# Where the split weights lie in on-chip memory, relative to the activation tiles, in a one-core decoder layer

## The chip, the cores and the metric

The kernel runs on one core of a Trainium2 chip. The core has TensorE (PE, the matrix engine), VectorE (DVE), ScalarE (ACT), GpSimd (POOL) and SyncE (SP), which only issues transfers here. The metric is the device time of one execution in microseconds (us). Lower is better.

## The reference

One layer of a decoder: 512 tokens, model width 2,048, everything in 32-bit floats.

```
mod = silu(c) @ w_ada + b_ada                     # six shift/scale/gate vectors
h = rmsnorm(x, g_mix) * (1 + sc1) + sh1
proj = h @ w_in          # q,k,v of 8 stick-breaking heads; q,k,v of 8 sparse heads;
                         # index queries, index key, index weights; two gates of 2048
y_a = stick_breaking_attention(q_a, k_a, v_a) @ w_a
y_b = sparse_attention(rope(q_b), rope(k_b), v_b, top 128 by the indexer) @ w_b
x = x + (1 + gt1) * ((sigmoid(g_a) * y_a + sigmoid(g_b) * y_b) @ w_o)
h = rmsnorm(x, g_ffn) * (1 + sc2) + sh2
u = causal_conv_width_3(h @ w_up)                 # 2 x 5632 channels
out = rmsnorm(x + (1 + gt2) * ((silu(u_a) * u_b) @ w_down), g_final)
```

Nearly all arithmetic is in the products with `w_in`, `w_a`, `w_b`, `w_o`, `w_up` and `w_down`.

## The kernel before

**Products in three parts.** Every operand of a large product is split into two `float32r` parts, a high one and the rest (`parts`, line 131, for weights, giving `wh` on ACT at line 133 and `wl` on DVE at line 135; `split`, line 160, for activations, into slots of tag `F`). `mm3` (line 141) then issues three matmuls: high by high (line 143), high by rest (144), rest by high (145). The second argument of `mm` is the stationary operand (128 columns, loaded as weights into the array), the third the moving one (256 or 512 columns). The profile names a matmul as out<-moving,stationary.

**Three ways to use them.**
- *Strassen units with tokens as columns* (`unit`, line 207): 31 of them for most of `w_in`, 8 for `w_o`, 41 for `w_up`. A unit makes two output tiles of 512 tokens with seven products instead of eight. The weights' parts are stationary and the token forms (`f`, halves of F tiles) are moving, 256 columns at a time: 7 x 8 x 3 matmuls.
- *Weights stationary, 512 tokens moving*: the first query products (from line 389), the 80-column tail (line 460), `w_a` and `w_b` (lines 926 and 968), and the first sixteen steps of the up-projection (`plain`, line 1108; some of these go over 256 columns).
- *Tokens stationary, 512 columns of weights moving*: the values (lines 440 to 448 and `values`, line 669), and all of `w_down` (`plain_down`, line 1230, and `strassen_down`, line 1282, Strassen units with tokens as rows). The very last `w_down` rows are split into F tiles beforehand (line 1419), so that there both operands are F tiles.

**Buffers.** `sb.tile(..., tag=...)` takes a buffer of a tag; tiles with one tag take turns on its `bufs` buffers. The buffers of a pool lie one behind the other in the order in which the tags are first used, each start rounded up to 32 bytes; a pool's first byte is 16,512 per partition here. So a 4-byte tile pushes everything behind it by 32 bytes. Before the change `eps` (4 bytes) stands ahead of the large tags, and `c_col` (64 bytes) stands between `raw` and `wl`. Worked out from the sizes, in bytes past a multiple of 512:

| tag | before |
|---|---|
| `T`, `F` (62 buffers of 2,048), `raw` (8 of 4,096) | 288 (32 past a multiple of 128) |
| `wl`, `wh` (3 buffers of 4,096 each) | 352 (96 past a multiple of 128) |
| `const` (identity, ones, masks) | 128 |

The column blocks of a weights' part are 512 bytes apart and the halves of an F tile 1,024, so every matmul of a full block has its two operands 64 bytes apart, modulo 512, wherever one is a weights' part. The tail's blocks are 80 columns, 320 bytes, apart.

**Order.** The instructions of an engine run in the order of its queue; the builder orders them by program order as their inputs and buffers come free. `behind(p)` adds that what is issued inside comes after `p` on the same engine. The transfer of the convolution's weights (`cw`, line 1087) goes out on ACT's queue behind `sig`, the last sigmoid of the input projection. `macc` (line 283) takes the row sums of the `w_ada` products that DVE makes beside the matmuls (`ada_half`, line 287); its last readers are `ada_end` (line 306) near the end of the `w_o` units. `cw` and `macc` are separate buffers.

Of the kernel before, what the change touches and what calls it, by code (L numbers as in the profile page):

```python
# [10 lines left out]
F32 = mybir.dt.float32  # L11
F32R = mybir.dt.float32r
# [6 lines left out]
P = 128  # L19
D = 2048  # L20
S = 512
KT = D // P
# [54 lines left out]
def block_kernel(ctx: ExitStack, tc: tile.TileContext, A: dict, out: bass.AP):  # L77
    nc = tc.nc
    sb = ctx.enter_context(tc.tile_pool(name="sb", bufs=1))
    pp = ctx.enter_context(tc.tile_pool(name="pp", bufs=1, space=PSUM))  # L80
    dr = ctx.enter_context(tc.tile_pool(name="dr", bufs=1, space=bass.MemoryType.DRAM))

# [33 lines left out]
    b_ada = vec[:, :96]  # L116
    g_mix, g_ffn = (vec[:, 96 + i * KT : 96 + (i + 1) * KT] for i in range(2))
    mask = sb.tile([P, 2, P], BF16, tag="mask", name="mask")
    cw = sb.tile([P, 2 * NJ, 4], F32, tag="cw", name="cw")
    eps = sb.tile([P, 1], F32, tag="eps", name="eps")  # L120
    nc.vector.memset(eps, EPS)


# [4 lines left out]

    pins = {}

    def parts(raw, w=1024):
        wh = t2k("wh", 3, F32R, w)
        pins["wh"] = act(wh, raw, AF.Copy)  # L133
        wl = t2k("wl", 3, F32R, w)
        pins["wl"] = tt(wl, raw, wh.bitcast(F32), ALU.subtract)  # L135
        return wh, wl

# [69 lines left out]
    def unit(src, f, between=lambda *_: None, late=None):  # L207

        n = len(f)
        w = n * P
        bank = (acc, att)[units[0] % 2]
        units[0] += 1
        r1, r2, r3 = (bank()[:, :HALF] for _ in range(3))

        def product(ps, a, name, first, pairs=None):
            for p in pairs or range(n):  # L220
                last = mm3(ps, cols(a, p), f[p][name], first and p == 0, p == n - 1, check=False)
            return last

        a11 = load(src[0], w)
        a21 = load(src[2], w)
        a22 = load(src[3], w)
        a12 = load(src[1], w)
        product(r1, parts(a11, w), "B11", True)
        e = t2k("ta", 2)
        p1, p5 = e[:, :HALF], e[:, HALF:]  # L230
        act(p1, r1, AF.Copy)
        s = t2k("raw", 8, w=w)
        last_v = tt(s, a21, a22, ALU.add)  # L233
        product(r3, parts(s, w), "T1", True)
        last = act(p5, r3, AF.Copy)
        between(0, last, last_v)
        tt(s, s, a11, ALU.subtract)  # L237
        product(r2, parts(s, w), "T2", True)
        e = t2k("sp", 2)
        u2, u3 = e[:, :HALF], e[:, HALF:]  # L240
        last_v = tt(u2, r2, p1, ALU.add)
        if late:
            c1, c2 = slot(), slot()
            steps = late(c1, c2)
            tt(s, a12, s, ALU.subtract)
            tt(a11, a11, a21, ALU.subtract)
            tt(u3, p1, p5, ALU.add)
            product(r3, parts(s, w), "B22", False)
            b21 = parts(a11, w), parts(a12, w)
            tt(c1[:, HALF:], r3, u2, ALU.add)  # L250
            next(steps)
            product(r2, b21[0], "T3", False)
            t4 = parts(a22, w)
            next(steps)
            tt(c2[:, HALF:], r2, u3, ALU.add)
            next(steps)
            product(r1, b21[1], "B21", False)
            act(c1[:, :HALF], r1, AF.Copy)
            next(steps)
            at = n - n // 3 - 1  # L260
            with behind(product(r2, t4, "T4", False, range(at))):
                last = next(steps)
            with behind(last):
                product(r2, t4, "T4", False, range(at, n))
            tt(c2[:, :HALF], r2, p1, ALU.add)
            return c1, c2
        product(r1, parts(a12, w), "B21", False)
        c1, c2 = slot(), slot()
        last = act(c1[:, :HALF], r1, AF.Copy)
        between(1, last, last_v)  # L270
        tt(a11, a11, a21, ALU.subtract)
        product(r2, parts(a11, w), "T3", False)
        tt(u3, r2, p1, ALU.add)  # L273
        tt(c2[:, HALF:], u3, p5, ALU.add)
        tt(a12, a12, s, ALU.subtract)
        product(r3, parts(a12, w), "B22", False)
        tt(c1[:, HALF:], r3, u2, ALU.add)
        product(r2, parts(a22, w), "T4", False)
        tt(c2[:, :HALF], r2, p1, ALU.add)
        return c1, c2  # L280


    macc = sb.tile([P, 96, 2], F32, tag="macc", name="macc")
    mod = sb.tile([P, 96], F32, tag="mod", name="mod")
    amp = sb.tile([P, 2, KT], F32, tag="amp", name="amp")

# [37 lines left out]
        return cb  # L324

    cb = c_spread()
    c_col = sb.tile([P, KT], F32, tag="c_col", name="c_col")
    nc.scalar.dma_start(c_col, A["c_col"])
    act(c_col, c_col, AF.Silu)

# [1 line left out]
    def rms(squares, blocks=range(NQB), bank=outs):  # L332

        total = bank()
        at = slice(blocks[0] * P, (blocks[-1] + 1) * P)
        for b in blocks:
            for i, t in enumerate(squares):
                mm(total[:, b : b + 1], t[:, b * P : (b + 1) * P], ones[:, :1], start=b == blocks[0] and i == 0,
                   stop=i == len(squares) - 1, skip_group_check=True)
        r = sb.tile([P, NQB], F32, tag="r", bufs=2, name=nm("r"))  # L340
        rb = r[:, blocks[0] : blocks[-1] + 1]
        act(rb, total[:, blocks[0] : blocks[-1] + 1], AF.Sqrt, scale=1.0 / D, bias=eps)
        nc.vector.reciprocal(rb, rb)
# [145 lines left out]

    def rope_tables():  # L490
        f0, f1, f2, f3, f123, f23, fr = _turn_parts()
        inv = sb.tile([64, 1], F32, tag="inv", name="inv")
        nc.scalar.dma_start(inv, A["inv_freq"])
        pos = t2k("T", 2, I32)[:64]
        nc.scalar.dma_start(pos, A["positions"].to_broadcast([64, S]))
# [199 lines left out]
    def indexer():  # L695
# [6 lines left out]
        for b in range(NQB):  # L702
            nc.tensor.transpose(wps[:, b * IDXH : (b + 1) * IDXH], tail[IDXD:TN, b * P : (b + 1) * P],
                                ident[IDXD:TN, IDXD:TN])
        wi = sb.tile([P, NQB, IDXH], F32, tag="wi", name="wi")
        nc.vector.tensor_copy(wi.rearrange("p b h -> p (b h)"), wps[:, : NQB * IDXH])
        bias.extend(slot()[:, : (b + 1) * P] for b in range(1, NQB))
        yield
# [36 lines left out]
        for b in range(1, NQB):  # L745
            sc = bias[b]
            for i in range(TOPK // 8):
                m8 = sb.tile([P, 8], F32, tag="m8", bufs=2, name=nm("m8"))
                nc.vector.max(out=m8, in_=sc)
                nc.vector.match_replace(out=sc, in_to_replace=m8, in_values=sc, imm_value=TAKEN)  # L750
                if i % 2:
                    yield
            ts(sc, sc, TAKEN, NEG, ALU.not_equal, ALU.mult)
# [127 lines left out]
    ya = [split(o) for o in ya]  # L881

    def sparse_1(q, k):
        m = sb.tile([P, NQB], F32, tag="m", bufs=2, name=nm("m"))
        s = sb.tile([P, NQB], F32, tag="s", bufs=2, name=nm("s"))
        soft = sb.tile([P, 10 * P], F32, tag="soft", name=nm("soft"))
        lg = strips(*(acc() for _ in range(3)))
        p = strips(*of_soft(soft))
        for b in (2, 0, 1, 3):
            W = (b + 1) * P  # L890
            mm(lg[b], q[:, b * P : (b + 1) * P], k[:, :W], start=b > 0, stop=True, skip_group_check=True)
        for b in (2, 0, 1, 3):
            nc.vector.tensor_tensor_reduce(out=p[b], in0=lg[b], in1=bias[b], scale=HD**-0.5, scalar=-3.0e38,
                                           op0=ALU.add, op1=ALU.max, accum_out=m[:, b : b + 1])
        last = ts(m, m, -1.0, None, ALU.mult)
        for b in (2, 0, 1, 3):
            act(p[b], p[b], AF.Exp, bias=m[:, b : b + 1], accum_out=s[:, b : b + 1])
        return p, s, last
# [115 lines left out]
    def norm_late(c1, c2):  # L1014
# [1 line left out]
        c, sq = (c1, c2), (t2k("ta", 2), t2k("sp", 2))  # L1016
        total, rstd = att(), outs()
        wide = t2k("T", 2)
        r = sb.tile([P, NQB], F32, tag="r", bufs=2, name=nm("r"))

        def add_up(t, blocks, first=False):
            for b in blocks:
# [60 lines left out]
    rstd, finish_left, *left_norm = norm2  # L1083


    with behind(sig):
        nc.scalar.dma_start(cw, A["conv"])
    yd = [dr.tile([P, 2 * S], F32, tag=f"yd{j}", name=f"yd{j}") for j in range(NJ // 2)]
# [349 lines left out]
        return [fetch(x1t[:, t, b * S : (b + 1) * S]) for b in range(2, 4)]  # L1438

    def finish_tokens(t, xs, s):  # L1440
        r = sb.tile([P, NQB], F32, tag="r", bufs=2, name=nm("r"))
# [13 lines left out]
    for t in range(NQB):  # L1455
        ahead = operands(t + 1) if t + 1 < NQB else None
        xs = []
        s = sb.tile([P, NQB], F32, tag="s", bufs=2, name=nm("s"))
        for b in range(4):
            if not ps:  # L1460
                ps = bank(t)
# [126 lines left out]
```

## Time and profile before

| | |
|---|---|
| three runs | 2758.18, 2774.71, 2789.82 us (median 2774.71) |
| profiled execution, its own time | 2759.24 us |
| its span, first to last instruction | 2757.5 us |
| PE busy, matmuls | 2697.6 us (98%), 18,704 |
| weight loads busy | 2457.7 us (89%) |
| DVE busy | 2411.3 us (87%) |
| ACT busy | 1450.7 us (53%) |
| moved | 550.08 MB, 199 GB/s |
| mean granted TensorE clock | 0.995 |

Busy times of PE are modelled at the ends, since matmuls overlap; what one matmul costs in a dense stretch is the distance between the starts of two. The page's counts of PE are those of matmul records; a product of plain 32-bit floats has two, a `float32r` product one. Stages by time, roughly: first query products to 100 us, values to 192, tail and single tiles to 237, Strassen units of `w_in` to 855, indexer, values and attention to 1175, `w_b` to 1262, `w_o` to 1445, up-projection to 2292, `w_down` to the end.

### The profile page before, as it was taken

The numbers are of one execution on the slowest core, as the hardware profiler recorded it, in microseconds if no ns is written. First come the engines' busy times: TensorE is split into PE (matmuls) and PEld (weight loads), VectorE is DVE, ScalarE is ACT, GpSimd is POOL, SyncE is SP. The second block draws the span as 40 slices with busy tenths as digits, with TensorE's granted clock in tenths as the row PEclk, the third lists the DMA queues.
The fourth block names the chain that finished last, engine by engine and source line by source line (L and its number), as shares of the span: only waits on it lengthen the run. The fifth ranks groups of instructions, "written<-read, shape, count | busy, mean of one in ns | idle before, by whom it ended". The sixth has DMA issues, their size and how long they took to land.

```text
span 2757.5 us, 47708 instructions
## 1 busy us (share of the span) xinstructions
PE 2697.6 (98%) x18704; PEld 2457.7 (89%) x18704; DVE 2411.3 (87%) x3452; ACT 1450.7 (53%) x2045; POOL 315.3 (11%) x519
## 2 busy tenths in 40 slices
PE   8999999999999999999999999999999999999997
PEld 6779999999998777879999999999999998887876
DVE  8978979988887899889879999999999997888886
ACT  4444454455556655434557555555555555546452
POOL 0010000000012011111230000000000000002122
PEclk9999999999999999999999999999999999999998
DMA  9973456756567467865783566666666446569786
GB/s 348 354 254 122 156 181 195 232 176 188 166 195 238 133 206 243 279 213 174 233 269 108 179 176 178 187 177 184 176 179 182 130 131 219 151 176 245 193 256 196
DMA packets 164189, 550.08 MB, mean 199 GB/s; under 512 B 21414, under 2 KB 21798, under 8 KB 163964
## 3 DMA queue, kind: packets, MB, share of 16 engines
q1 hardware_dynamic: 116220, 405.34, 45.9%
q0 software_dynamic: 47152, 141.30, 18.4%
q8 instruction: 147, 2.41, 0.4%
q14 instruction: 78, 0.64, 0.1%
q10 hardware_dynamic: 592, 0.39, 0.1%
HBM read 453.71 MB, written 89.83 MB: 197 GB/s over the span
## 4 chain that ended last, share of the span: by engine, by line
PE 67%; DVE 8%; DMA 5%; issue 4%; ACT 1%; POOL 0%; DVEq 0%; POOLq 0%; ACTq 0%; SPq 0%
PE att L145 10%; PE att L143 10%; PE att L144 10%; PE acc L145 10%; PE acc L143 10%; PE acc L144 10%; DVE wl L135 3%; DMA raw<-in_w_x 1%; DMA raw<-in_w_down 1%; PE acc L722 1%; PE acc L816 1%; PE outs L922 1%; DMA raw<-in_w_o 1%; PE outs L145 1%; PE outs L144 1%
## 5 line engine op out<-in xcount | busy, mean ns | idle before, releaser
L133 ACT ACTIVATE wh<-raw 128x1024 fp32r<-128x1024 f32 (+2 forms) x792 | 828.9, 1053 | 962.2 <-DVE raw L237 179.1
L135 DVE TENSOR_TENSOR wl<-raw,wh 128x1024 fp32r<-128x1024 f32 (+2 forms) x792 | 952.6, 1210 | 126.5 <-ACT wh L133 121.8
L143 PE MATMUL acc<-F,wh 128*128 128x256 f32 (+1 forms) x2464 | 709.1, 290 | 12.8 <-ACT wh L133 7.1
L145 PE MATMUL acc<-F,wl 128*128 128x256 f32 (+1 forms) x2464 | 710.6, 289 | 6.1 <-DVE wl L135 6.1
L144 PE MATMUL acc<-F,wh 128*128 128x256 f32 (+1 forms) x2464 | 710.3, 288 | 0.6 <-DVE F L388 0.4
L143 PE MATMUL att<-F,wh 128*128 128x256 f32 (+1 forms) x2448 | 704.8, 289 | 5.8 <-DVE sp L273 4.5
L145 PE MATMUL att<-F,wl 128*128 128x256 f32 (+1 forms) x2448 | 704.2, 288 | 3.3 <-DVE wl L135 3.0
L144 PE MATMUL att<-F,wh 128*128 128x256 f32 (+1 forms) x2448 | 704.5, 288 | 1.2 <-DVE F L164 1.2
L143 PEld LDWEIGHTS acc<-F,wh 128*128 128x128 f32 x2464 | 463.3, 188 | 29.5 <-ACT wh L133 12.2
L145 PEld LDWEIGHTS acc<-F,wl 128*128 128x128 f32 x2464 | 463.0, 188 | 19.2 <-DVE wl L135 8.5
L143 PEld LDWEIGHTS att<-F,wh 128*128 128x128 f32 x2448 | 460.4, 188 | 19.3 <-ACT wh L133 5.2
L144 PEld LDWEIGHTS acc<-F,wh 128*128 128x128 f32 x2464 | 463.8, 188 | 12.9 <-DVE F L388 1.4
L144 PEld LDWEIGHTS att<-F,wh 128*128 128x128 f32 x2448 | 461.3, 188 | 13.6 <-DVE F L164 4.3
L145 PEld LDWEIGHTS att<-F,wl 128*128 128x128 f32 x2448 | 460.3, 188 | 14.3 <-DVE wl L135 5.0
L290 DVE SCALAR_TENSOR_TENSOR raw<-raw,raw 128x1024 f32<-128x1024 f32 x152 | 182.1, 1217 | 0.0
L143 PE MATMUL att<-wh,F 128*128 128x512 f32 x448 | 178.5, 399 | 0.2 <-ACT wh L133 0.2
L145 PE MATMUL att<-wh,F 128*128 128x512 f32 x448 | 176.3, 394 | 0.0
L144 PE MATMUL att<-wl,F 128*128 128x512 f32 x448 | 176.1, 393 | 0.2 <-DVE wl L135 0.2
L233 DVE TENSOR_TENSOR raw<-raw,raw 128x1024 f32<-128x1024 f32 x80 | 97.4, 1218 | 42.3 <-DMA raw<-in_w_x 24.3
L144 PE MATMUL acc<-wl,F 128*128 128x512 f32 x288 | 114.0, 396 | 2.4 <-DVE wl L135 2.4
L145 PE MATMUL acc<-wh,F 128*128 128x512 f32 x288 | 113.7, 395 | 0.0
L143 PE MATMUL acc<-wh,F 128*128 128x512 f32 x288 | 112.2, 392 | 0.0
(364 smaller groups left out, 3621.3 us busy)
## 6 DMA issues: line engine op xcount, KB each, us to landing
raw<-in_w_up SPq DMA_DIRECT2D x164, 512.0 KB, 4.0
raw<-in_w_ada SPq DMA_DIRECT2D x152, 512.0 KB, 5.2
raw<-in_w_x SPq DMA_DIRECT2D x128, 512.0 KB, 4.3
raw<-in_w_down SPq DMA_DIRECT2D x104, 512.0 KB, 5.3
xd<-F POOLq DMA_DIRECT2D x64, 256.0 KB, 2.5
F<-xd POOLq DMA_DIRECT2D x64, 256.0 KB, 4.7
raw<-in_w_o SPq DMA_DIRECT2D x32, 512.0 KB, 5.1
soft<-in_w_gate SPq DMA_DIRECT2D x32, 512.0 KB, 4.1
```

The source lines that it names most:

```text
L133: pins["wh"] = act(wh, raw, AF.Copy)
L135: pins["wl"] = tt(wl, raw, wh.bitcast(F32), ALU.subtract)
L143: mm(ps, ah, bh, start=first, stop=False, skip_group_check=not check)
L144: mm(ps, ah, bl, start=False, stop=False, skip_group_check=not check)
L145: return mm(ps, al, bh, start=False, stop=last, skip_group_check=not check)
L233: last_v = tt(s, a21, a22, ALU.add)
L290: return stt(raw, raw, 1.0, cb[half], ALU.mult, ALU.mult, accum_out=macc[:, t, half : half + 1])
L722: mm(dots[:, :W], both[:, b * P : (b + 1) * P], kiR[i][:, :W], start=i == 0, stop=i == 1)
L816: mm(o, negtri if tri else negones, i, start=False, stop=True, skip_group_check=True)
L922: mm(o[:, b * P : (b + 1) * P], vs[kb][:, hd % 4 * HD : (hd % 4 + 1) * HD], pT[b][:, kb * P : (kb + 1) * P], start=kb == 0, stop=kb == b)
```

## The change

The small tiles (`eps`, `c_col`, `r`, `inv`, `wi`, `m8`, `m`, `s`) move into a pool of their own, `tiny`, so that they no longer stand between the large buffers. `cw` and `macc` share one buffer (tag `macc`, 1,408 bytes): `cw` can be filled only when `macc` has been read for the last time. The buffers of `wh` and `wl` grow by 128 bytes to 4,224, and `parts` gets an argument `off`: the part begins `off` elements into its buffer. `unit` passes `OFF = 16` (64 bytes) for its seven products; all other callers (`prep`, `strassen_down`) leave it at 0.

By the sizes, in bytes past a multiple of 512: `T`, `F` and `raw` begin at 0; the three `wl` buffers at 0, 128 and 256; the three `wh` buffers at 384, 0 and 128. So in units a part begins 64 bytes past a multiple of 128 and the F tiles on one, and in all other products both begin on a multiple of 128.

No instruction is added or removed, and no shape changes.

```diff
     sb = ctx.enter_context(tc.tile_pool(name="sb", bufs=1))
+    tiny = ctx.enter_context(tc.tile_pool(name="tiny", bufs=1))
...
-    cw = sb.tile([P, 2 * NJ, 4], F32, tag="cw", name="cw")
-    eps = sb.tile([P, 1], F32, tag="eps", name="eps")
+    eps = tiny.tile([P, 1], F32, tag="eps", name="eps")
...
-    def parts(raw, w=1024):
-        wh = t2k("wh", 3, F32R, w)
+    OFF = 16
+
+    def parts(raw, w=1024, off=0):
+        wh = t2k("wh", 3, F32R, 1024 + 2 * OFF)[:, off : off + w]
         pins["wh"] = act(wh, raw, AF.Copy)
-        wl = t2k("wl", 3, F32R, w)
+        wl = t2k("wl", 3, F32R, 1024 + 2 * OFF)[:, off : off + w]
         pins["wl"] = tt(wl, raw, wh.bitcast(F32), ALU.subtract)
         return wh, wl
...
-        product(r1, parts(a11, w), "B11", True)
+        product(r1, parts(a11, w, OFF), "B11", True)
...
-    macc = sb.tile([P, 96, 2], F32, tag="macc", name="macc")
+    macc = sb.tile([P, 2 * NJ * 4], F32, tag="macc", name="macc")[:, :192].rearrange("p (t h) -> p t h", h=2)
...
-    c_col = sb.tile([P, KT], F32, tag="c_col", name="c_col")
+    c_col = tiny.tile([P, KT], F32, tag="c_col", name="c_col")
...
-        r = sb.tile([P, NQB], F32, tag="r", bufs=2, name=nm("r"))
+        r = tiny.tile([P, NQB], F32, tag="r", bufs=2, name=nm("r"))
...
     rstd, finish_left, *left_norm = norm2
 
+    cw = sb.tile([P, 2 * NJ, 4], F32, tag="macc", name="cw")
     with behind(sig):
         nc.scalar.dma_start(cw, A["conv"])
```

The other small tiles (`inv`, `wi`, `m8`, `m`, `s`) change from `sb` to `tiny` in the same way.

More of the change, by code (lines that the diff above doesn't have):

```diff
@@ L233, in unit @@
         last_v = tt(s, a21, a22, ALU.add)
-        product(r3, parts(s, w), "T1", True)
+        product(r3, parts(s, w, OFF), "T1", True)
         last = act(p5, r3, AF.Copy)
@@ L237, in unit @@
         tt(s, s, a11, ALU.subtract)
-        product(r2, parts(s, w), "T2", True)
+        product(r2, parts(s, w, OFF), "T2", True)
         e = t2k("sp", 2)
@@ L247, in unit @@
             tt(u3, p1, p5, ALU.add)
-            product(r3, parts(s, w), "B22", False)
-            b21 = parts(a11, w), parts(a12, w)
+            product(r3, parts(s, w, OFF), "B22", False)
+            b21 = parts(a11, w, OFF), parts(a12, w, OFF)
             tt(c1[:, HALF:], r3, u2, ALU.add)
@@ L252, in unit @@
             product(r2, b21[0], "T3", False)
-            t4 = parts(a22, w)
+            t4 = parts(a22, w, OFF)
             next(steps)
@@ L266, in unit @@
             return c1, c2
-        product(r1, parts(a12, w), "B21", False)
+        product(r1, parts(a12, w, OFF), "B21", False)
         c1, c2 = slot(), slot()
@@ L271, in unit @@
         tt(a11, a11, a21, ALU.subtract)
-        product(r2, parts(a11, w), "T3", False)
+        product(r2, parts(a11, w, OFF), "T3", False)
         tt(u3, r2, p1, ALU.add)
@@ L275, in unit @@
         tt(a12, a12, s, ALU.subtract)
-        product(r3, parts(a12, w), "B22", False)
+        product(r3, parts(a12, w, OFF), "B22", False)
         tt(c1[:, HALF:], r3, u2, ALU.add)
-        product(r2, parts(a22, w), "T4", False)
+        product(r2, parts(a22, w, OFF), "T4", False)
         tt(c2[:, :HALF], r2, p1, ALU.add)
         return c1, c2
-    macc = sb.tile([P, 96, 2], F32, tag="macc", name="macc")
+    macc = sb.tile([P, 2 * NJ * 4], F32, tag="macc", name="macc")[:, :192].rearrange("p (t h) -> p t h", h=2)
     mod = sb.tile([P, 96], F32, tag="mod", name="mod")
@@ L491, in rope_tables @@
         f0, f1, f2, f3, f123, f23, fr = _turn_parts()
-        inv = sb.tile([64, 1], F32, tag="inv", name="inv")
+        inv = tiny.tile([64, 1], F32, tag="inv", name="inv")
         nc.scalar.dma_start(inv, A["inv_freq"])
@@ L704, in indexer @@
                                 ident[IDXD:TN, IDXD:TN])
-        wi = sb.tile([P, NQB, IDXH], F32, tag="wi", name="wi")
+        wi = tiny.tile([P, NQB, IDXH], F32, tag="wi", name="wi")
         nc.vector.tensor_copy(wi.rearrange("p b h -> p (b h)"), wps[:, : NQB * IDXH])
@@ L747, in indexer @@
             for i in range(TOPK // 8):
-                m8 = sb.tile([P, 8], F32, tag="m8", bufs=2, name=nm("m8"))
+                m8 = tiny.tile([P, 8], F32, tag="m8", bufs=2, name=nm("m8"))
                 nc.vector.max(out=m8, in_=sc)
@@ L883, in sparse_1 @@
     def sparse_1(q, k):
-        m = sb.tile([P, NQB], F32, tag="m", bufs=2, name=nm("m"))
-        s = sb.tile([P, NQB], F32, tag="s", bufs=2, name=nm("s"))
+        m = tiny.tile([P, NQB], F32, tag="m", bufs=2, name=nm("m"))
+        s = tiny.tile([P, NQB], F32, tag="s", bufs=2, name=nm("s"))
         soft = sb.tile([P, 10 * P], F32, tag="soft", name=nm("soft"))
@@ L1018, in norm_late @@
         wide = t2k("T", 2)
-        r = sb.tile([P, NQB], F32, tag="r", bufs=2, name=nm("r"))
+        r = tiny.tile([P, NQB], F32, tag="r", bufs=2, name=nm("r"))
         def add_up(t, blocks, first=False):
@@ L1440, in finish_tokens @@
     def finish_tokens(t, xs, s):
-        r = sb.tile([P, NQB], F32, tag="r", bufs=2, name=nm("r"))
+        r = tiny.tile([P, NQB], F32, tag="r", bufs=2, name=nm("r"))
         tt(r[:, :2], s[:, :2], s[:, 2:], ALU.add)
@@ L1457, in block_kernel @@
         xs = []
-        s = sb.tile([P, NQB], F32, tag="s", bufs=2, name=nm("s"))
+        s = tiny.tile([P, NQB], F32, tag="s", bufs=2, name=nm("s"))
         for b in range(4):
```

## The prediction

> **What bounds the kernel now.** I read the page first: busy times and the chain that ended last.
>
> ```profile
> span 2757.5 us, 47708 instructions
> ...
> PE 2697.6 (98%) x18704; PEld 2457.7 (89%) x18704; DVE 2411.3 (87%) x3452; ACT 1450.7 (53%) x2045; POOL 315.3 (11%) x519
> ...
> PE 67%; DVE 8%; DMA 5%; issue 4%; ACT 1%; POOL 0%; DVEq 0%; POOLq 0%; ACTq 0%; SPq 0%
> ```
>
> TensorE works through 98% of the span and carries two thirds of the chain. VectorE follows at 87%. So what counts is how long one matmul keeps the next one waiting, unless a stage waits for something else. The stretches of 100 us say which do (columns: PE, weight loads, DVE, ACT, POOL with counts, clock, DMA share, GB/s):
>
> ```profile
> 0.00:100.00 100.00, 87.72 (x350) 67.02 (x350) 85.61 (x162) 41.35 (x58) 2.78 (x7) 1.00 0.94 341
> 1800.00:1900.00 100.00, 100.00 (x884) 100.00 (x884) 93.98 (x111) 56.38 (x73) 7.64 (x11) 1.00 0.66 182
> ```
>
> The first 100 us wait for transfers (DMA 0.94, PE 88%); in the up-projection PE never stops. Next, the groups by shape, to count the matmuls that read a weights' part (wh or wl). The form is out<-moving,stationary.
>
> ```profile
> L143 PE MATMUL acc<-F,wh 128*128 128x256 f32 x2240 | 623.3, 278 | 3.4 <-DVE sp L273 2.2 <-DVE F L977 0.5 <-ACT wh L133 0.3
> ...
> L143 PE MATMUL att<-wh,F 128*128 128x512 f32 x448 | 178.5, 399 | 0.2 <-ACT wh L133 0.2
> ...
> L144 PE MATMUL acc<-wl,F 128*128 128x512 f32 x288 | 114.0, 396 | 2.4 <-DVE wl L135 2.4
> ...
> L144 PE MATMUL att<-F,wh 128*128 128x512 f32 x208 | 84.4, 406 | 1.2 <-DVE F L164 1.2
> ...
> L145 PE MATMUL outs<-wh,F 128*128 128x512 f32 x96 | 37.8, 393 | 0.5 <-DVE F L438 0.5
> ```
>
> Each row stands for three lines of `mm3` and the first and fourth for two banks. That makes three kinds: 6 x 2,240 = 13,440 of 256 columns in the Strassen units (tokens moving, weights stationary); 3 x (448 + 288 + 96) = 2,496 of 512 columns with the weights moving; 6 x 208 = 1,248 of 512 columns with the weights stationary. The mean durations here are modelled and hold the overlap, so I don't use them. What a matmul costs is the distance from one start to the next, and the view of one source line gives it: count, first and last start in stretches without waits. In this order: units (two stretches), weights moving, weights stationary, and the last products of all, whose two operands are both F tiles.
>
> ```profile
> L143 PE MATMUL acc<-F,wh x442: 276/276/276, 1701.8 to 1985.0; 128*128 128x256 f32 x148
> L143 PE MATMUL att<-F,wh x435: 276/276/281, 1718.8 to 1999.7; 128*128 128x256 f32 x145
> ```
> ```profile
> L143 PE MATMUL acc<-F,wh x112: 281/281/281, 296.6 to 355.6; 128*128 128x256 f32 x112
> L143 PE MATMUL att<-F,wh x87: 281/281/281, 289.8 to 359.8; 128*128 128x256 f32 x87
> ```
> ```profile
> L143 PE MATMUL att<-wh,F x80: 388/388/392, 2329.8 to 2450.0; 128*128 128x512 f32 x80
> L143 PE MATMUL acc<-wh,F x72: 388/388/392, 2344.2 to 2447.2; 128*128 128x512 f32 x72
> L143 PE MATMUL outs<-wh,F x24: 388/388/397, 2346.3 to 2447.9; 128*128 128x512 f32 x24
> ```
> ```profile
> L143 PE MATMUL acc<-F,wh x58: 393/396/398, 1209.6 to 1249.5; 128*128 128x512 f32 x58
> ```
> ```profile
> L143 PE MATMUL att<-F,F x16: 389/389/389, 2717.3 to 2727.5; 128*128 128x512 f32 x16
> L143 PE MATMUL acc<-F,F x14: 389/389/389, 2713.2 to 2735.6; 128*128 128x512 f32 x14
> L143 PE MATMUL outs<-F,F x8: 389/389/389, 2714.6 to 2738.4; 128*128 128x512 f32 x8
> ```
>
> Every L143 opens a group of three. Units: 297.9 us / 876 / 3 = 113.4 ns; in the other stretch 70.0 / 198 / 3 = 117.8 ns. Weights moving: 120.2 / 175 / 3 = 229.0 ns. Weights stationary: 39.9 / 57 / 3 = 233.3 ns. Both operands F: 25.2 / 37 / 3 = 227.0 ns. The three 512-column kinds have one shape and one data type and differ by up to 6.3 ns. What differs is where the operands lie: by the tile sizes (kernel section) the weights' parts begin 64 bytes off the F tiles, modulo 512, while two F tiles are in step.
>
> **The change part by part.** *In step for all but the units.* If the in-step pair of F tiles shows what 512 columns cost in step, the weights-moving kind falls from 229.0 to 227.0: 2,496 x 2.0 = 5.0 us. The weights-stationary kind falls from 233.3 to 227.0. Of its 1,248, the 16 x 7 x 3 = 336 of the first query products lie in the first 100 us, where the transfers end last, and bring nothing; 912 x 6.3 = 5.7 us. Both lie on PE's path in stages where PE is the chain, and shorten no group by over 3%, so DVE (87%) doesn't come up behind it. Bounds: the saving is between 0 (the position is not what sets them apart) and these 10.7 us. I take 10.7, because the F pair is the nearest row, with the 80-column products as the doubt (rivals). The first up-projection products of 256 columns (at most 16 x 6 x 3 x 2 = 576 by the code) also go in step; no row shows 256 columns in step, so by the two rows of the units 576 x 4.4 ns = 2.5 us either way; I take 0.
>
> *Units stay 64 bytes off.* Modulo 128 their relative position is what it was, so they keep 113.4 ns, with stretches of 117.8. What is new is that the weights' buffers now lie 0, 128 and 256 bytes (wl) and 384, 0 and 128 (wh) past a multiple of 512, and all F tiles on one. I take 0; the bounds are a rival each.
>
> *The splits.* ACT and DVE write and read the parts at other offsets. The two rows below are a subtraction whose operands are 64 bytes apart and one whose operands are in step:
>
> ```profile
> L135 DVE TENSOR_TENSOR wl<-raw,wh 128x1024 fp32r<-128x1024 f32 x758 | 918.2, 1219 | 113.9 <-ACT wh L133 109.4
> ...
> L237 DVE TENSOR_TENSOR raw<-raw,raw 128x1024 f32<-128x1024 f32 x80 | 97.7, 1222 | 1.2
> ```
>
> 1,219 against 1,222 ns: no effect to expect on DVE, 0 us (between -3 and +3 ns on each of 758: 2 us either way).
>
> *The convolution's weights in macc's buffer.* Today their transfer is issued on ACT's queue long before they are read:
>
> ```profile
> L1092 ACT ACTIVATE w<-F,cw x88: 795/802/831, 1500.2 to 2296.3; 128x512 f32<-128x512 f32 x88
> ...
> L1087 ACTq DMA_DIRECT2D cw<-in_conv x1: 335/335/335, 860.4 to 860.4; - x1
> ...
> DMA to landing us min/median/max: 4.9/4.9/4.9
> ```
> ```profile
> 1400.56 0.18 DVE L306 TENSOR_TENSOR mod<-macc 128x32 f32<-128x32 f32 x1
> ```
> ```profile
> 1400.60 1.06 ACT L133 ACTIVATE wh<-raw 128x1024 fp32r<-128x1024 f32 x1 [1.66 <-PE acc L144]
> ```
>
> Now it must wait for macc's last reader, L306 at 1400.6, so it moves past ACT's and DVE's work of 540 us. It lands at about 1406, 94 us before L1092 first reads: that slack covers it. If ACT reaches the issue before L306 ends, ACT stands still, behind it the next split (L133), and behind that DVE's wl and PE. ACT idles 1.7 us before such a split, so I take 0, and 0 to 3 us as the bounds; if the cover were gone it would be one late split, not a stage. SP's and POOL's queues see no change, and the small tiles in their own pool cost nothing.
>
> **The sum.** -5.0 - 5.7 = about -11 us. The profiled execution took 2759.2 us (its span and 1.7 around it): 2748. The median of the three runs shown is 2774.7, 0.56% above it, so 2748 x 1.0056 = 2764; I forecast 2763. The runs spread over 32 us (2758 to 2790). The two rhythms of the units can make that: all of them slow rather than fast would be 13,440 x 4.4 ns = 59 us.
>
> **Rivals.**
> *A. In step is not what makes the F pair fast; nothing moves (0.17).* For it, the 80-column products, whose weights advance by 320 bytes from one group of three to the next:
>
> ```profile
> 200.04 0.40 PE L143 MATMUL acc<-F,wh 128*80 128x512 f32 x1
> ...
> 200.75 0.40 PE L143 MATMUL acc<-F,wh 128*80 128x512 f32 x1
> ...
> 202.12 0.39 PE L143 MATMUL acc<-F,wh 128*80 128x512 f32 x1
> 202.35 0.39 PE L144 MATMUL acc<-F,wh 128*80 128x512 f32 x1
> ...
> 202.80 0.40 PE L143 MATMUL acc<-F,wh 128*80 128x512 f32 x1
> ...
> 203.51 0.39 PE L143 MATMUL acc<-F,wh 128*128 128x512 f32 x1
> ```
>
> From 200.04 (fourth block) and from 202.80 (eighth) a group takes 0.71 us; these are in step modulo 256 (64 + 3 x 320 = 4 x 256). From 202.12 (seventh, 192 off) it takes 0.68. So here in step is the slowest, and the rhythm repeats after four blocks, not two: 128 bytes may not be the whole period. Against it, 37 groups of F pairs in a row at 0.681. If these blocks rule, the stationary kind goes to 0.71 / 3 = 236.7 ns: 912 x 3.4 = +3 us, against -5 from the other kind: 2757, or 2773 in the median's terms. The Trainium skill speaks for no effect at all: "TensorE: Matmul & The Clock Gate", section "Step-by-step: what each phase is for", has two independent read ports, so that loading the next weights takes nothing from the running matmul. By that rule the sum would be 0. The trace does not bear it out as it stands, since equal shapes stand at 227.0 and 233.3 ns.
>
> *B. The units fall into the slow rhythm; slower (0.13).* With buffers 128 bytes apart, half of the weights lie 192 instead of 64 off modulo 256, and where a product goes from one buffer to the next, a fast rhythm may break. Up to 13,440 x 4.4 = 59 us, less the 3 us of the stretch shown slow, less 11: 2759 + 45 = 2804, median's terms 2820. It ends slower than before as soon as a fifth of the units more are slow (11 / 59). For it: the long fast stretch never changed its position. Against it: modulo 128 nothing changes.
>
> *C. The 32-byte start itself costs time (0.13).* All operands of these products begin 32 bytes past a multiple of 64, and will begin on one. A run of 256 columns (1,024 bytes) then touches 16 pieces of 64 bytes instead of 17: 113.4 x 16 / 17 = 106.7 ns; 512 columns 32 instead of 33: 220. That would be 13,440 x 6.7 + 3,744 x 7 = 116 us. But DVE is busy 93.98 of 100 us there, so about 6% can go before DVE becomes the bound; I put 100 us and the 11 on top: 2648, or 2663. Against it: 227.0 is twice 113.4, which a cost per run would not give (33 is not twice 17), but a cost per 64 bytes streamed would, and that stays. The same page of the Trainium skill (section "Back-to-back issue gap") puts 262 cycles on 256 columns and 518 on 512 when warm, estimated 109 and 216 ns; by it about 4 and 11 ns a matmul would be open to such a gain.
>
> *D. The units stay fast throughout (0.09).* The slow stretches go: some 10 to 25 us more, 2740 to 2750 in the median's terms.
>
> **How the numbers follow.** My forecast has 0.48, with its own range 2748 to 2780 by the runs' spread; A 0.17, B 0.13, C 0.13, D 0.09. I leave out C and the upper half of B (2 in 10) and take 2725 to 2792. A measurement of this kernel tells about 1% from no change, 28 us. Faster by more: C, most of D and a tenth of the forecast where the runs fall low, 0.27. Slower by more: the upper part of B, 0.09. Within: 0.64.
>
> **What would show it.** In the changed profile's source line view: weights moving at 227 instead of 229 ns, weights stationary at 227 instead of 233.3, units at 113.4 with or without stretches at 117.8; the convolution's transfer just behind L306 and no PE wait there. I am wrong if the units leave 113.4 in their long stretch in the up-projection, or if either 512-column kind stays or rises.

## The result, and the profile after

| | before | after |
|---|---|---|
| median of 20 runs each | 2776.12 us | 2760.09 us |
| lowest to highest | 2758.18 to 2795.25 us | 2752.71 to 2764.96 us |
| profiled execution, its own time | 2759.24 us | 2762.39 us |

The ratio is 0.995, with a 95% interval of 0.9931 to 0.997: 16 us, most of it from the upper end. The slowest runs came down by 30 us, the fastest by 5. The profiled execution of before happened to lie at its lower end, so the two profiles alone show no gain at all. The page of after, its span, busy times and chain:

```profile
span 2760.6 us, 47709 instructions
...
PE 2696.7 (98%) x18704; PEld 2455.3 (89%) x18704; DVE 2409.9 (87%) x3452; ACT 1448.9 (52%) x2045; POOL 315.1 (11%) x519
...
PE 70%; DVE 7%; DMA 4%; issue 3%; ACT 1%; POOL 0%; DVEq 0%; ACTq 0%; POOLq 0%; SPq 0%
```

Nothing has moved between the engines: PE is 0.9 us less busy and still carries the chain. (The one instruction more is a semaphore wait on SyncE.) The order of the instructions is the same on every engine but for the transfer of `cw`, so what differs is where the operands lie. The view of one source line again, of after, for the same stretches as before the change (L145 is now the first line of a group of three): units in the up-projection, units early, weights moving, weights stationary, both operands F.

```profile
L145 PE MATMUL att<-F,wh x444: 275/276/281, 1715.8 to 1999.8; 128*128 128x256 f32 x148
L145 PE MATMUL acc<-F,wh x433: 275/276/277, 1701.8 to 1982.0; 128*128 128x256 f32 x145
...
L145 PE MATMUL acc<-F,wh x112: 275/276/358, 297.2 to 354.8; 128*128 128x256 f32 x112
L145 PE MATMUL att<-F,wh x87: 275/276/357, 289.8 to 359.9; 128*128 128x256 f32 x87
...
L145 PE MATMUL att<-wh,F x78: 390/393/398, 2329.6 to 2449.4; 128*128 128x512 f32 x78
L145 PE MATMUL acc<-wh,F x72: 390/394/398, 2342.1 to 2445.9; 128*128 128x512 f32 x72
L145 PE MATMUL outs<-wh,F x24: 392/393/398, 2344.2 to 2446.6; 128*128 128x512 f32 x24
...
L145 PE MATMUL acc<-F,wh x58: 388/393/401, 1209.8 to 1249.6; 128*128 128x512 f32 x58
...
L145 PE MATMUL acc<-F,F x18: 388/389/390, 2712.8 to 2738.0; 128*128 128x512 f32 x18
L145 PE MATMUL att<-F,F x16: 388/389/390, 2719.6 to 2729.8; 128*128 128x512 f32 x16
L145 PE MATMUL outs<-F,F x6: 389/389/390, 2716.9 to 2739.4; 128*128 128x512 f32 x6
```

Worked as in the prediction (last start minus first, by groups less one, by three): the long stretch of units is at 298.0 / 876 / 3 = 113.4 ns, as before. Weights moving went **up**, from 229.0 to 119.8 / 173 / 3 = 230.8. Weights stationary went from 233.3 to 39.8 / 57 / 3 = 232.7, not to 227. F pairs are where they were (26.6 / 39 / 3 = 227.4). In the early stretch the median of a unit's matmul fell from 281 to 276, so the slow rhythm is gone, yet the count from 290 to 360 us is 199 groups as before. The waits of PE there, of after, say why (before had none there):

```profile
PE att L145 <- DVE sp L275: 1.7, 1, 1.7
PE acc L145 <- DVE sp L275: 0.2, 1, 0.2
```

A faster PE waits for VectorE in that place, and the gain is handed back.

The step with `cw`, in the view of that tile and in the timeline of VectorE, of after:

```profile
L1095 ACT ACTIVATE w<-F,cw x88: 796/801/837, 1498.1 to 2293.6; 128x512 f32<-128x512 f32 x88
...
L1090 ACTq DMA_DIRECT2D cw<-in_conv x1: 333/333/333, 1397.4 to 1397.4; - x1
...
DMA to landing us min/median/max: 5.2/5.2/5.2
```
```profile
1396.70 0.19 DVE L308 TENSOR_TENSOR mod<-macc 128x32 f32<-128x32 f32 x1
```

The transfer goes out 0.7 us after `macc`'s last reader starts and lands 95 us before its first use, as forecast, and no PE wait is there.

### The profile page after: what moved, and what is told of

The parts are those of the page before. It is cut to its first block, busy times and chain, and to the rows that moved or that the text cites. A ratio compares the mean times of both kernels' runs of the same rounds, so it can differ in the third digit from the quotient of the medians.

```text
span 2760.6 us, 47709 instructions
## 1 busy us (share of the span) xinstructions
PE 2696.7 (98%) x18704; PEld 2455.3 (89%) x18704; DVE 2409.9 (87%) x3452; ACT 1448.9 (52%) x2045; POOL 315.1 (11%) x519
## 4 chain that ended last, share of the span: by engine, by line
PE 70%; DVE 7%; DMA 4%; issue 3%; ACT 1%; POOL 0%; DVEq 0%; ACTq 0%; POOLq 0%; SPq 0%
PE att L145 11%; PE att L147 11%; PE att L146 10%; PE acc L145 10%; PE acc L147 10%; PE acc L146 10%; DVE wl L137 2%; DMA raw<-in_w_x 1%; PE acc L724 1%; PE acc L818 1%; PE outs L924 1%; PE outs L147 1%; PE outs L146 1%; PE outs L145 1%; PE acc L893 1%
## 5 line engine op out<-in xcount | busy, mean ns | idle before, releaser
L145 PE MATMUL acc<-F,wh 128*128 128x256 f32 (+1 forms) x2464 | 707.3, 289 | 14.0 <-ACT wh L135 7.2
L147 PE MATMUL acc<-F,wl 128*128 128x256 f32 (+1 forms) x2464 | 709.5, 288 | 5.4 <-DVE wl L137 5.3
L145 PE MATMUL att<-F,wh 128*128 128x256 f32 (+1 forms) x2448 | 703.6, 288 | 7.7 <-DVE sp L275 7.6
L147 PE MATMUL att<-F,wl 128*128 128x256 f32 (+1 forms) x2448 | 703.7, 288 | 3.8 <-DVE wl L137 3.8
L145 PEld LDWEIGHTS acc<-F,wh 128*128 128x128 f32 x2464 | 462.5, 188 | 31.0 <-ACT wh L135 12.2
L145 PEld LDWEIGHTS att<-F,wh 128*128 128x128 f32 x2448 | 460.7, 188 | 21.4 <-ACT wh L135 7.4
L147 PEld LDWEIGHTS acc<-F,wl 128*128 128x128 f32 x2464 | 462.3, 188 | 18.5 <-DVE wl L137 8.1
L147 PEld LDWEIGHTS att<-F,wl 128*128 128x128 f32 x2448 | 460.3, 188 | 14.0 <-DVE wl L137 5.2
L145 PE MATMUL att<-wh,F 128*128 128x512 f32 x448 | 179.8, 402 | 0.2 <-ACT wh L135 0.2
L147 PE MATMUL att<-wh,F 128*128 128x512 f32 x448 | 175.8, 393 | 0.0
L145 PE MATMUL acc<-wh,F 128*128 128x512 f32 x288 | 114.1, 399 | 1.8 <-ACT wh L135 1.8
L147 PE MATMUL acc<-wh,F 128*128 128x512 f32 x288 | 113.7, 395 | 0.0
```

Of the source, the lines that this page charges most:

```text
L145: mm(ps, ah, bh, start=first, stop=False, skip_group_check=not check)
L147: return mm(ps, al, bh, start=False, stop=last, skip_group_check=not check)
```

## The experiments

In the tables below, a distance is the mean over all pairs of successive matmuls of a kind with no wait between them (under 127 ns for 256 columns, under 250 for 512), worked out from the starts in the trace. The **excess** of the units is the sum of their distances over 113.33 ns, the fast rhythm (340 ns a group). A position is the start of the weights' part minus the start of the F tile, modulo 256 bytes; in units a triple gives it for the three matmuls of a group. The column of the units counts all 256-column products, with the up-projection's first ones (315 of 13,725 pairs); that of the weights-stationary matmuls counts the tail's with 80 columns.

By the sizes, the buffers of after lie 4,224 bytes apart, so `wh` and `wl` of one product differ by 128 modulo 256. In step modulo 128 is then not in step modulo 256: of the 512-column products some matmuls stand at 0 and some at 128, and the units' triples go from buffer to buffer in the order (192, 192, 64), (64, 64, 192), (192, 192, 64), so that of three products in a row two stand alike. Two things were open: whether the period is 128 or 256 bytes, or in step is worthless; and whether the gain comes from the aligned starts, the shared buffer of `cw`, or this staggering of buffers.

**One position for all products.** Four kernels with unpadded buffers (4,096 bytes), so that all parts stand at one position; `c_col` takes up the difference. The first leaves it in `tiny`, the others give it 16, 32 or 48 elements in `sb`. Against after:

```diff
-    OFF = 16
+    OFF = 0
...
-        wh = t2k("wh", 3, F32R, 1024 + 2 * OFF)[:, off : off + w]
+        wh = t2k("wh", 3, F32R, 1024)[:, off : off + w]
...
-    c_col = tiny.tile([P, KT], F32, tag="c_col", name="c_col")
+    c_col = sb.tile([P, 16], F32, tag="c_col", name="c_col")[:, :KT]
```

(`wl` likewise; the last pair is that of position 64.)

> The changed kernel with no offset in any product and weights' buffers of 4,096 bytes: every large buffer begins on a multiple of 512, all operands in step modulo 512. Theory 1 (the forecast's: in step is what makes the F pair cost 227): both 512-column kinds at 227 ns. Theory 2 (the position modulo 128 is not what sets the cost; the last F pair is fast for another reason): at least one of them stays above 229. Units in step: by the changed kernel's few in-step 256-column products (118 to 119 ns) 118, that is 13,440 x 4.6 = 60 us slower than all fast, near 2,800 us.

> As the one before, with c_col's 64 bytes back between raw and wl: weights' parts 64 bytes off modulo 512 in every product, as before the change, but every start on a multiple of 64. Theory 3 (the gain comes from the start on a multiple of 64, which keeps the units out of their slow rhythm): units at 113.4 to 113.9 ns, runs within 15 us of each other, median near 2,760. Theory 4 (the gain comes from the buffers' different distances, so not from the start): slow stretches at 117.8 in the units, runs spread over 30 us as before, median near 2,775. Both: 512-column kinds at 229 and 233 as before.

> The pad is 128 bytes: all weights' parts 128 off modulo 512. If 128 bytes is the period (theory 1), every kind costs what it costs in step. If the period is longer (theory 2), it differs from in step by 2 ns or more in at least one kind; by the changed kernel's groups the weights-moving kind would then be slower than in step or than 64 off (229 to 233).

> The pad is 192 bytes: all weights' parts 192 off modulo 512. Period 128: the same as 64 off in every kind. Longer period: by the 80-column blocks of before (0.68 us a group at 192 off) the weights-stationary kind near 227 instead of 233, and the units perhaps without a slow rhythm: 912 x 6 = 5 us for the first, up to 15 for the second, median 2,755 to 2,760.

| position | median (lowest to highest), us | ratio, 95% | units, ns (excess, us) | 512, weights moving | 512, weights stationary |
|---|---|---|---|---|---|
| 0 | 2808.89 (2807.25 to 2810.9) | 1.0146, 1.0101 to 1.0191 | 119.97 (90.7) | 227.1 | 227.4 |
| 64 | 2784.39 (2769.65 to 2790.81) | 1.0052, 1.0023 to 1.008 | 116.05 (37.0) | 229.2 | 233.2 |
| 128 | 2812.48 (2810.3 to 2815.93) | 1.0163, 1.0108 to 1.0218 | 118.73 (73.8) | 232.5 | 232.4 |
| 192 | 2796.46 (2793.87 to 2799.14) | 1.0101, 1.0056 to 1.0146 | 117.1 (51.5) | 233.3 | 229.1 |

The view of one source line, position 0, then position 64 (units; weights moving, for position 0 alone; weights stationary):

```profile
L145 PE MATMUL att<-F,wh x431: 283/283/284, 1701.8 to 1997.8; 128*128 128x256 f32 x144
L145 PE MATMUL acc<-F,wh x398: 283/283/284, 1715.9 to 1999.9; 128*128 128x256 f32 x199
...
L145 PE MATMUL att<-wh,F x78: 389/389/396, 2345.3 to 2449.4; 128*128 128x512 f32 x78
L145 PE MATMUL acc<-wh,F x58: 389/389/389, 2361.7 to 2448.1; 128*128 128x512 f32 x58
L145 PE MATMUL outs<-wh,F x18: 389/389/389, 2363.7 to 2442.6; 128*128 128x512 f32 x18
...
L145 PE MATMUL acc<-F,wh x59: 389/389/389, 1210.3 to 1249.7; 128*128 128x512 f32 x59
```
```profile
L145 PE MATMUL acc<-F,wh x437: 281/281/282, 1701.8 to 1994.4; 128*128 128x256 f32 x146
L145 PE MATMUL att<-F,wh x407: 281/281/282, 1717.7 to 1999.7; 128*128 128x256 f32 x136
...
L145 PE MATMUL acc<-F,wh x57: 393/393/398, 1210.1 to 1249.3; 128*128 128x512 f32 x57
```

And position 128, then position 192, weights stationary in the same stretch:

```profile
L145 PE MATMUL acc<-F,wh x58: 390/393/404, 1210.0 to 1249.8; 128*128 128x512 f32 x58
```
```profile
L145 PE MATMUL acc<-F,wh x59: 388/388/388, 1209.8 to 1249.6; 128*128 128x512 f32 x59
```

At position 0 both 512-column kinds come down to what the F pairs show (moving 104.1 / 153 / 3 = 226.8, stationary 39.4 / 58 / 3 = 226.4): in step does what the prediction said of it. The units pay for it: 298.1 / 828 / 3 = 120.0 ns, without a fast rhythm anywhere. Positions 0 and 128 differ (226.4 against 39.8 / 57 / 3 = 232.7 ns), and so do 64 and 192 (39.2 / 56 / 3 = 233.3 against 39.8 / 58 / 3 = 228.7), so the period is not 128. Position 64 with aligned starts has what before has with starts 32 bytes past 64: both rhythms (here 297.9 / 843 / 3 = 117.8), 229 and 233.3. An aligned start by itself is worth nothing. It came out 0.5% slower than before, in the share of the slow rhythm; whether alignment changes that share, or the programs merely differ in it, these runs don't tell. What was expected of position 192 held for the weights-stationary kind only in part (229.1 ns, not 227) and failed for the units: they have long slow stretches, 51.5 us of excess, and the kernel took 2796 us instead of 2,755 to 2,760.

**Where the gain of after comes from.** Two kernels from before, both with starts still 32 bytes past 64: one that only lets `cw` take `macc`'s buffer, and one that also widens the buffers of the parts by 128 bytes, so that they are staggered as in after but 64 or 192 off everywhere. Beside the second ran after and, a single time, before, both unchanged. Against before:

```diff
-    cw = sb.tile([P, 2 * NJ, 4], F32, tag="cw", name="cw")
...
-        wh = t2k("wh", 3, F32R, w)
+        wh = t2k("wh", 3, F32R, 1056)[:, :w]
...
-    macc = sb.tile([P, 96, 2], F32, tag="macc", name="macc")
+    macc = sb.tile([P, 2 * NJ * 4], F32, tag="macc", name="macc")[:, :192].rearrange("p (t h) -> p t h", h=2)
...
+    cw = sb.tile([P, 2 * NJ, 4], F32, tag="macc", name="cw")
     with behind(sig):
```

(`wl` likewise; the middle pair is left out where only the buffer is shared.)

> The kernel before with two parts of the change alone: the weights' buffers grow by 128 bytes, and cw shares macc's buffer, which makes room for it. All small tiles stay where they were, so every operand still begins 32 bytes past a multiple of 64, and the weights' parts lie 64 or 192 bytes off modulo 256 in all products, the high and the low part of a pair differently. Theory 4 (the buffers' different distances keep the units out of the slow rhythm, the start on a multiple of 64 does nothing): units near 113.7 ns as after the change, runs within 15 us, median about 2,760. Theory 3 (the start counts): long slow stretches, runs spread over 30 us.

> The changed kernel itself, on the same chip as the others. All theories: units 113.5 to 114, median 2,755 to 2,765, runs within 15 us.

> The kernel before, a second profiled execution. If its spread comes from the two rhythms of the units, the time of this execution follows from the share of units in the slow one: 2,748 us for none and about 60 us more for all.

> The kernel before with one part alone: cw shares macc's buffer, buffers of 4,096 bytes, nothing moved off its 64 bytes. Theory 4 (the gain is the high and the low part lying at different distances): units with long stretches at 117.8 in some executions, runs spread over 25 us or more, ratio to before 0.997 to 1.003. If the sharing itself were the gain: median near 2,757 and runs within 15 us.

| kernel | median (lowest to highest), us | ratio, 95% | units, ns (excess, us) | moving | stationary |
|---|---|---|---|---|---|
| staggered, not aligned | 2755.74 (2753.32 to 2765.14) | 0.9946, 0.9913 to 0.9979 | 113.60 (3.7) | 231.1 | 231.7 |
| after, again | 2757.71 (2754.51 to 2766.84) | 0.9952, 0.9921 to 0.9982 | 113.81 (6.4) | 230.6 | 232.6 |
| before, again, one execution | 2759.67 | | 114.39 (14.5) | 229.4 | 233.2 |
| only `cw` in `macc` | 2773.44 (2759.97 to 2779.2) | 0.9994, 0.9961 to 1.0026 | 115.36 (27.7) | 229.1 | 233.2 |

The stagger alone gives the whole gain of after. Sharing the buffer gives none, and alignment, which the staggered kernel lacks, isn't needed.

Two executions of before, the profiled one and this second one, show what the runs' spread is made of. The view of the line L143 from 580 to 690 us, of the first and of the second:

```profile
L143 PE MATMUL att<-F,wh x163: 276/276/357, 594.2 to 689.9; 128*128 128x256 f32 x163
L143 PE MATMUL acc<-F,wh x154: 276/276/357, 579.9 to 672.5; 128*128 128x256 f32 x154
```
```profile
L143 PE MATMUL att<-F,wh x157: 281/281/281, 595.0 to 689.7; 128*128 128x256 f32 x157
L143 PE MATMUL acc<-F,wh x155: 281/281/281, 579.8 to 673.8; 128*128 128x256 f32 x155
```

The same program, the same operands, the same stretch: mostly fast in the one, slow throughout in the other. The times of these two don't show it: the second has 3.8 us more excess, and PE's waits inside the units take 5.0 us less (26.0 against 31.0), so it took 2759.67 us where the excess alone would have given some 2,763. No execution of before near its upper end was profiled, so the slow case comes from another kernel. The execution of the kernel with the shared buffer at 2775.26 us, 16 us above the profiled one of before, has the long stretch of the up-projection in the slow rhythm. Its view of the line (L142 there), then the stretch from 1700 to 2290 us of it and of before (columns as in the prediction):

```profile
L142 PE MATMUL acc<-F,wh x434: 281/281/281, 1702.0 to 1993.5; 128*128 128x256 f32 x145
L142 PE MATMUL att<-F,wh x410: 281/281/281, 1716.9 to 1999.9; 128*128 128x256 f32 x137
```
```profile
1700.00:2290.00 590.00, 590.00 (x5027) 586.03 (x5026) 536.42 (x631) 322.58 (x411) 37.69 (x56) 1.00 0.59 163
```
```profile
1700.00:2290.00 590.00, 590.00 (x5174) 586.04 (x5173) 550.52 (x651) 329.31 (x423) 38.22 (x57) 1.00 0.60 167
```

PE is busy all the time in both, and does 147 matmuls less in the first: 147 x 114.0 ns = 16.8 us. The excess of the units says the same, 27.7 - 10.7 = 17.0 us. So the spread of the old arrangement is, as far as these executions show it, mainly the share of its units that happens to run in the slow rhythm.

**Both at once.** In step modulo 256 for all but the units, and in units `wh` at 64 and `wl` at 192. That needs buffers a multiple of 256 bytes larger; the room comes from letting `cw` share the buffer of the attention's constants. Against after:

```diff
-        wh = t2k("wh", 3, F32R, 1024 + 2 * OFF)[:, off : off + w]
+        wh = t2k("wh", 3, F32R, 1024 + 64)[:, off : off + w]
...
-        wl = t2k("wl", 3, F32R, 1024 + 2 * OFF)[:, off : off + w]
+        wl = t2k("wl", 3, F32R, 1024 + 64)[:, 3 * off : 3 * off + w]
...
+    const2 = sb.tile([P, 3, P], F32, tag="conv", name="const2")
...
-    cw = sb.tile([P, 2 * NJ, 4], F32, tag="macc", name="cw")
+    cw = sb.tile([P, 2 * NJ, 4], F32, tag="conv", name="cw")
```

> The changed kernel with buffers 4,352 bytes apart, so that all begin in step with F modulo 256; in units the high part is 64 and the low part 192 bytes off, elsewhere both are in step modulo 256. (Room for it: macc is as small as before, cw shares a buffer with the attention's constants, which come in a transfer of their own.) If the position modulo 256 is all that counts: 512-column kinds at 227.0 to 227.4 as in p0, which is 2,448 x 3.4 + 1,392 x 5.1 = 15 us less than after the change; units at 113.5 to 113.9 as after; median about 2,745. If the period is 512 or the absolute position counts, one of the kinds stays above.

It took 2742.28 us (2740.65 to 2745.75), ratio 0.9885 (0.9837 to 0.9934), and beat after by 15.4 us beside it. Units 113.62 ns (excess 3.9), moving 227.2, stationary 227.4. The view of the line (L147 there), units and weights stationary:

```profile
L147 PE MATMUL att<-F,wh x445: 276/276/281, 1701.9 to 1986.2; 128*128 128x256 f32 x149
L147 PE MATMUL acc<-F,wh x432: 276/276/276, 1719.9 to 1999.8; 128*128 128x256 f32 x144
...
L147 PE MATMUL acc<-F,wh x75: 389/389/389, 1174.6 to 1224.9; 128*128 128x512 f32 x75
```

So 113.4 ns and 50.3 / 74 / 3 = 226.6 ns stand side by side. The period is not 512 either: with buffers 4,352 bytes apart the parts stand at 0 in one buffer and at 256 in the next, modulo 512, and the weights-moving matmuls take 227.2 and 227.1 ns there. The profile of after beside it (2755.65 us) gives the sum: units -2.5, weights moving -8.3, weights stationary -6.8, PE's waits in these kinds +2.2 us, together -15.4; the two profiles differ by 14.9. Against the kernel with position 0, the units give 90.7 - 3.9 = 86.8 us, and PE's waits inside them take 17.6 back (30.1 against 12.5): 69.2, and the executions differ by 67.7. A fifth of what PE gains in the units is lost to waits.

One more step on this gives the 256-column products of the up-projection's first steps the units' offsets too (`prep` passes `off`; in `plain` for every other step):

> best1, and the 256-column products of the first up-projection steps take the units' offsets (high part 64, low part 192) instead of standing in step. By 119.8 ns in step against 113.5 in the units: 324 x 6.3 = 2 us less than best1, median 2,738 to 2,743. All else as best1.

2741.86 us (2738.47 to 2746.39), ratio 0.9896 (0.9864 to 0.9928), excess of the units 2.3. The 1.6 us of excess less can't be told from nothing in the times.

**What ends the slow rhythm.** Two kernels made from the one with both at once. The first exchanges the offsets of `wh` and `wl` (a group stands at 192, 192, 64, always). The second gives both parts one offset, 64 and 192 by turns from product to product:

```diff
+    turn_of = [OFF]
...
+        if off:
+            turn_of[0] = 4 * OFF - turn_of[0]
+            off = turn_of[0]
         wh = t2k("wh", 3, F32R, 1024 + 64)[:, off : off + w]
...
-        wl = t2k("wl", 3, F32R, 1024 + 64)[:, 3 * off : 3 * off + w]
+        wl = t2k("wl", 3, F32R, 1024 + 64)[:, off : off + w]
```

> best1 with the two offsets of the units exchanged: high part 192, low part 64 bytes off. If it is the difference within a group of three that keeps the fast rhythm: units at 113.4 to 113.8 and the time of best1 (2,742) within 5 us. If the order counts: stretches at 117.8 and runs spread over 15 us.

> best1, but in units the high and the low part of one product have the same offset, 64 and 192 bytes by turns from product to product. If the fast rhythm needs the difference within a group of three: slow stretches at 117.8 as in p64 and p192, median 2,755 to 2,785. If a change of position every 24 matmuls is enough to end a slow stretch: units under 114.5 and median under 2,750. 512-column kinds at 227 in both.

Exchanged: 2779.77 us (2758.05 to 2785.07), ratio 0.9998 (0.9962 to 1.0034); the slow rhythm is back, at 298.2 / 836 / 3 = 118.9 ns, excess 55.6 (its line L147):

```profile
L147 PE MATMUL acc<-F,wh x420: 278/279/280, 1701.8 to 1991.0; 128*128 128x256 f32 x140
L147 PE MATMUL att<-F,wh x417: 278/278/280, 1711.8 to 2000.0; 128*128 128x256 f32 x139
```

By turns: 2744.48 us (2742.89 to 2746.14), ratio 0.9891 (0.9829 to 0.9952), excess 6.9, although constant 64 and constant 192 each had long slow stretches above. Its timeline, the first matmuls of groups where a stretch begins slow (start, duration):

```profile
1674.73 0.28 PE L151 MATMUL att<-F,wh 128*128 128x256 f32 x1
1675.08 0.28 PE L151 MATMUL att<-F,wh 128*128 128x256 f32 x1
1675.43 0.28 PE L151 MATMUL att<-F,wh 128*128 128x256 f32 x1
1675.77 0.28 PE L151 MATMUL att<-F,wh 128*128 128x256 f32 x1
1676.11 0.28 PE L151 MATMUL att<-F,wh 128*128 128x256 f32 x1
```

The first product, at 192, ends with the group that starts at 1675.08: 0.35 us a group up to there. The next product, at 64, begins at 1675.43, and a group takes 0.34 us from its first on. The table has every border between two products of units, eight groups each, without a wait from three groups ahead of it to six behind it. The rhythm ahead is that of the last three groups, the rhythm behind that of the third to the fifth:

| kernel | border | was slow: stays, turns fast | was fast: stays, turns slow |
|---|---|---|---|
| by turns | 192 to 64 | 0, 27 | 213, 0 |
| by turns | 64 to 192 | 11, 0 | 229, 0 |
| after | (192, 192, 64) to (64, 64, 192) | 0, 14 | 147, 0 |
| after | (64, 64, 192) to (192, 192, 64) | none | 160, 1 |
| after | (192, 192, 64) to itself | 9, 0 | 150, 0 |
| exchanged | (192, 192, 64) to itself | 369, 0 | 129, 0 |

The slow rhythm, once in, lives through any number of products at the same position and ends at the first border at which `wh` goes from 192 to 64. The fast one survives all of these borders but one of 1,029. With positions that change, a slow start lasts some 60 matmuls at most in after and 48 by turns, against some 970 in the profiled execution of before, 3,900 with only the buffer shared and 4,740 at position 64.

Two limits of this. A step from 192 to 64 between two matmuls is not enough: exchanged has one in every group, from `wh` to `wl`, and stays slow. And in after the product behind such a border is always a (64, 64, 192), which sheds the slow rhythm without any border: in the two kernels that have it in all products no slow stretch is longer than 12 matmuls. So the borders of after don't tell the step from the triple; those of by turns do, since at a constant 64 the slow rhythm stays.

## Why the prediction was right, and where it was wrong

The time was right by luck: 2763 forecast, 2760.09 measured, inside the range. The sum behind it was not: both of its terms, the two 512-column kinds, failed, and a rival's gain of about the same size stood in for them. By the prediction's own sign ("if either 512-column kind stays or rises") its account was wrong: one rose, and the other all but stayed.

*In step, -5.0 us (weights moving).* Wrong. The rows show 230.8 ns in place of 227.0, a loss; by the excess over 226.67 ns it went from 6.0 to 9.3 us over all of these matmuls. The premise that failed is that a part and an F tile that both begin on a multiple of 128 are in step as two F tiles are. The mechanism held: at 0 modulo 256 the kind falls to 227, as the F pairs said. After puts 44% of the matmuls there and the others at 128, where a whole kernel measured 232.5. The mean by these shares is 230.1 ns; over all of them it measured 230.6.

*In step, -5.7 us (weights stationary).* Wrong for the same reason: 232.7 in place of 227.0, 0.8 us gained (excess 8.6 to 7.8). Here the shares are not enough: 44% stand at 0 too, which would give 230.2 ns. By the starts in the trace of after, two in a row at 0 are 227.9 ns apart, one at 0 and the next at 128 are 233.7, one at 128 and the next at 0 are 233.0, and two at 128 are 233.0; only 148 of 1,278 pairs are of the first sort. Why the change of position within a group costs as much as standing at 128, no run shows. The kernel with both at once has the two terms at their size and more: against before, 6.0 - 1.2 = 4.8 us and 8.6 - 1.0 = 7.6 us, the second over more matmuls than the 912 of the forecast.

*Units, 0.* The figure 113.4 held, and the stretches at 117.8, which the forecast let stand as they were, went. This is rival D, given 0.09 and priced at 10 to 25 us. Between an execution of the old arrangement at its usual time (2775.26 us, the kernel with only the buffer shared) and the profiled one of after (2762.39): units 27.7 - 6.6 = -21.1 us, the 512-column kinds +2.5, PE's waits inside the three kinds +5.6, together -13.0; measured -12.9. The forecast had seen that the two rhythms make the spread of the runs, and had the price, 59 us for all units; it took them as given. What it missed is that a change of position can end a slow rhythm.

*First up-projection products, 0.* At position 0, 256 columns take 120.0 ns; in after they stand partly at 0 and partly at 128, 118.3 to 119.0 ns, some 5 ns over the fast rhythm and 1 over the slow: a loss of some 1.5 us by the 306 pairs of them that follow one another, inside the 2.5 allowed.

*Splits, 0; convolution's weights, 0.* Held: DVE's busy time is 2409.9 against 2411.3 us, and the kernel with only the shared buffer is at 0.9994.

*Rival A* (in step isn't what makes the F pair fast) falls with position 0. What spoke for it, the 80-column products with a period of four blocks, was the right hint: 128 bytes is not the period. But they don't follow the order of the 128-column weights: in the kernel with position 0, too, by the starts in its trace, two of them in a row in step are 236 to 237 ns apart, and two at 192 are 226 to 227. So the order found for 128 columns doesn't hold for a stationary operand of 80. The rule of the Trainium skill beside it ("TensorE: Matmul & The Clock Gate", "Step-by-step: what each phase is for": two independent read ports, so loading the next weights takes nothing from the running matmul) would, as the prediction reads it, have all four positions equal; they stand at 227.1 to 233.3 ns and, at 256 columns, at 116.1 to 120.0.

*Rival B* (units fall into the slow rhythm where they go from buffer to buffer) is the reverse of what happened: going from buffer to buffer is what ends it. Where the position never changes B's size is real: 37.0 us of excess at 64, 51.5 at 192.

*Rival C* (the 32-byte start) falls with position 64: aligned, and no faster.

## What to carry to other kernels

Where PE never waits, compare the start-to-start distances of equal matmuls before tuning anything else: here 6% of a 256-column matmul and 3% of a 512-column one hung on where two operands lie relative to each other, modulo 256 bytes, and the best position for one shape was the worst for the other. Check padding against the full period: 128 bytes of it put more than half of the 512-column matmuls at another position than the forecast meant. And when runs of one program spread by 1%, look for one stretch that runs at two rhythms in two executions before calling it noise; a single profile of before can be the lucky one.

## What the runs showed of the hardware that was not expected

- Where a kernel has one position for all products, the 512-column distances go by the start of the moving operand minus that of the stationary one, modulo 256: 227 ns at 0, 229 at 64, 232.5 at 128, 233.3 at 192. Weights moving at 64 and weights stationary at 192 agree (229.2 and 229.1), as do the other two (233.3 and 233.2). The period is neither 128 nor 512. Where the position changes within a group, as in after, weights stationary take 232.6 ns, more than the 230.2 of a mean by shares.
- At 256 columns the order is another: 120.0 ns at 0 and 118.7 at 128, each with one rhythm; at 64 and at 192 two rhythms, 113.3 and 117.8.
- Which of the two rhythms a stretch gets differs from execution to execution, and at a constant position it holds to the stretch's end. Of the steps from one product to the next, only that of `wh` from 192 to 64 was seen to end the slow one; why that step, and why (64, 64, 192) throughout never stays slow while (192, 192, 64) throughout does, stays open.
- Even at their best, 256 and 512 columns take 113.3 and 227 ns, at any alignment of the starts tried. The Trainium skill ("TensorE: Matmul & The Clock Gate", "Back-to-back issue gap") gives 262 and 518 cycles for the isolated gap of one matmul, estimated 109 and 216 ns at its 2.4 GHz. No row of these kinds here comes down to that, at a granted clock of 1.00.
